# Experts' weight ring: the eleven early buffers first, loaded unit by unit during the output projection

## The chip, the core and the metric

The kernel runs on one NeuronCore of a Trainium2 chip, as one launch. The metric is the device time of that core in microseconds, taken as the median of several executions. The engines named below are TensorE (PE; PEld is its weight load), VectorE (DVE), ScalarE (ACT), GpSimd (POOL) and SyncE (SP), which here only issues DMAs. Each engine works through its own list of instructions in order, so an instruction that waits holds up all that stand behind it on the same engine.

## What is computed

Two transformer blocks in a row on 512 tokens of width 1024. The change touches the last part of the second block: the output projection of the token mixer, the second norm, and a mixture of 32 experts of which each token uses two. Cut to that:

```python
def second_block(x, c, ...):
    ...
    x = x + g1 * token_mixer(h, ...)              # ends in: merged @ w_out
    h = rms_norm(x, norm2_g) * (1.0 + sc2) + sh2
    x = x + g2 * hier_moe(h, ...)
    return rms_norm(x, final_g)

def hier_moe(h, w_group, b_group, w_expert, b_expert, w_gate, w_up, w_down):
    g_prob = softmax(h @ w_group + b_group)       # 4 groups, best one
    e_logits = h @ w_expert + b_expert            # 8 experts of that group, best two
    ...
    def expert_block(xb, e):
        return (silu(xb @ w_gate[e]) * (xb @ w_up[e])) @ w_down[e]
```

All in float32. An expert has three matrices (gate and up 1024x256, down 256x1024) of 1.05 MB each, 32 experts have 96 of them.

## The kernel before

**Stages.** `block2` runs the second block. Its last stages are `Moe.mix_out` (output projection, residual, norm, router logits), `Moe.route` (which token goes to which expert, by one-hot matmuls) and `Moe.run` (the experts). The 32 experts are taken as 16 pairs, then one block for an expert with more than 64 tokens (the "far" block, the thirteenth in the order, three matrices), so 17 blocks with 99 matrices.

**The ring of weights.** Each matrix is loaded into one unit of 128x2048 float32, by one DMA on SP's queue. There are 18 units, which `Moe.raw` hands out in turn: `NR = 5, 11` says that the first 5 come from the pool `er2`, the next 11 from the pool `er`, and the last 2 are the halves of `x`, the residual stream, which is free once its rows are stored. `er` is opened in `Moe.__init__`, before the output projection. `er2` can be opened only when the projection's input `m_hi`, `m_lo` has been read (`mst.close()`), and `block2` puts it at the head of the list. A pair needs 6 units: gate, gate, up, up, down, down. With 18 units three pairs fit; from the nineteenth load on a unit must be given back by the pair three places earlier: gate and up when `up` of that pair is through on PE, down when `down` is.

**Loads.** `Moe.load` takes the units of a pair at once, first gate and up of both experts and then both down, so in the first pair five units are of `er2` and one (a down) is of `er`. The first pair is asked for in `Moe.open`, the next two at the head of `Moe.run`. The loads of the third pair are placed behind `self.hold`. At the first load that comes round to a used unit, POOL clears two words of it (`memset`), placed behind the first gather.

**Hold.** `self.hold` is a small DMA on SP's queue that stores one column (128 words) of the first gathered block. It waits for the first gather, so SP issues nothing behind it until that has landed.

**Gather.** The normed tokens are stored to `hd` in DRAM, four stores of 128 rows, the last one at the end of `mix_out`. The first gather (POOL, indirect) reads rows of `hd` and so waits for all four stores and for the indices. The three blocks that gathers fill, `xg`, and the tiles `h` that are stored to `hd` rotate through the same three buffers `wraw`; the fourth `h` takes the buffer of the first.

**Order.** The order on each engine is made by a scheduler when the kernel is built; `tc.issue_after(i)` keeps what is written under it behind instruction `i`. `declare_no_dep` and the rest are untouched here. DMAs of SP take turns on eight completion semaphores, so an issue also waits until the transfer eight issues earlier has landed.

Of the kernel before, what the change touches and what calls it, by code (L numbers as in the profile page):

```python
# [9 lines left out]
F32 = mybir.dt.float32  # L10
# [1879 lines left out]
NE = 32  # L1890
# [1 line left out]
FAR = 128  # L1892
NPAIR = NE // 2
NOV = 15
NR = 5, 11
NX = 3
AHEAD = 2
FAR_AT = 12
# [6 lines left out]
class Moe:  # L1905
# [3 lines left out]
    def __init__(self, K, st):  # L1909

        nc, i = K.nc, K.i
        self.K, self.sc = K, []
        P = lambda *a, **k: st.enter_context(K.pool(*a, **k))
        cp = self.cp = P(name="ec", bufs=1, side="right")
        self.x = cp.tile([128, NT, D], F32, name="xres2")
        self.ss = cp.tile([128, 2, NT], F32, name="ss2")
        self.er = [P(name="er", bufs=NR[1], side="right")]
        self.nraw = 0
        self.first = None
        self.cst = cp.tile([128, ECOLS], F32, name="ecst")  # L1920
        nc.sync.dma_start(self.cst, i["ce"])
        self.xa = K.dram.tile([T, D], F32, name="xa")

        self.yd = K.dram.tile([2 * T, D], F32, name="yd")
# [11 lines left out]
    def mix_out(self, xd, mod, m_hi, m_lo):  # L1936

        K, cp, x, ss = self.K, self.cp, self.x, self.ss
        nc, i = K.nc, K.i
# [5 lines left out]
        with K.pool(name="mo", bufs=2) as wp:  # L1945
# [56 lines left out]
            def logits1(t):  # L2002
                ps = K.aux()
                for k in range(4):
                    s = slice(k * 128, (k + 1) * 128)
                    nc.tensor.transpose(ps[:, s], x[:, t, 512 + k * 128:640 + k * 128], K.ident)
                h = K.wraw()
                late = t >= NT - 2
                (nc.vector if t == NT - 1 else nc.gpsimd).tensor_mul(h, x[:, t, :], G)
                v = K.col(1, "msv")  # L2010
                nc.vector.tensor_add(v, ss[:, 0, t:t + 1], ss[:, 1, t:t + 1])
                nc.vector.tensor_scalar(v, v, RS / D, RS * 1e-6, op0=OP.mult, op1=OP.add)
                xT = rot([128, 512], "xT")
                nc.scalar.copy(xT, ps)
                rs = K.rsqrt(v, 1)
                nc.vector.scalar_tensor_tensor(l0[:, t], l0[:, t], rs, bias, op0=OP.mult, op1=OP.add)
                pl = K.aux()
                for k in range(4):
                    nc.tensor.matmul(pl[:, :36], xT[:, k * 128:(k + 1) * 128], wr[:, 4 + k, :],
                                     start=k == 0, stop=k == 3)  # L2020
                nc.vector.scalar_tensor_tensor(self.lg[:, t], pl[:, :36], rs, l0[:, t], op0=OP.mult, op1=OP.add)
                if late:

                    dg = rot([128, 128], "dg")
                    nc.scalar.activation(dg, K.ident, AF.Copy, scale=rs)
                    for s in HALF:
                        ps = K.mm()
                        nc.tensor.matmul(ps, dg, h[:, s], start=True, stop=False)
                        nc.tensor.matmul(ps, K.ident, sh2[:, s], start=False, stop=True)
                        nc.scalar.copy(h[:, s], ps)  # L2030
                else:
                    nc.scalar.activation(h, h, AF.Copy, scale=rs)
                    nc.gpsimd.tensor_add(h, h, sh2)
                nc.sync.dma_start(self.hd[t * 128:(t + 1) * 128, :], h)

            wt = []
            for u in range(4):
                raw = K.wraw()
                r3 = raw.rearrange("p (k n) -> p k n", k=2)
                nc.sync.dma_start(r3, w[u * 256:(u + 1) * 256, 512:].rearrange("(k p) n -> p k n", p=128))  # L2040
                wt.append(K.split(raw, pool=None if u < 3 else wp, bufs=3 if u < 3 else 1))
            for t in range(NT):
                if t == 1:
                    logits0()
                if t > 1:
                    logits1(t - 2)
                ps = K.mm()
                for k in range(8):
                    hi, lo = (a[:, (k % 2) * 512:(k % 2 + 1) * 512] for a in wt[k // 2])
                    tt = slice(t * 128, (t + 1) * 128)  # L2050
                    nc.tensor.matmul(ps, m_hi[:, k, tt], hi, start=k == 0, stop=False)
                    nc.tensor.matmul(ps, m_hi[:, k, tt], lo, start=False, stop=False)
                    nc.tensor.matmul(ps, m_lo[:, k, tt], hi, start=False, stop=k == 7)
                residual(1, t, ps)
# [3 lines left out]
    def route(self):  # L2058
        K, cp = self.K, self.cp
        nc, tc, i = K.nc, K.tc, K.i  # L2060
# [13 lines left out]
        with K.pool(name="eh", bufs=2, side="right") as hp, ExitStack() as late:  # L2074
# [89 lines left out]
            q1 = places(rk, iota, "roh")  # L2164
            at = index(idx[:, :NPAIR], slots(q1, hb)[:, :NPAIR], T).ins
            self.gather(self.xg[0], idx[:, 0:1])

            self.hold = nc.sync.dma_start(K.dram.tile([128, 1], F32, name="hold"), self.xg[0][:, 0:1]).ins
            late.enter_context(tc.issue_after(at))

            def softmax(src, m, n, nm):
# [86 lines left out]
    def gather(self, xb, ixc):  # L2258

        nc = self.K.nc  # L2260
        at = nc.gpsimd.indirect_dma_start(out=xb, out_offset=None, in_=self.hd,
                                          in_offset=bass.IndirectOffsetOnAxis(ap=ixc, axis=0),
                                          bounds_check=T - 1, oob_is_err=False)
        self.first = self.first or at.ins

    def load(self, *experts):

        nc = self.K.nc
        rw = [[self.raw() for _ in range(2)] for _ in experts]
        rw = [(*a, self.raw()) for a in rw]  # L2270
        for a, b, n in [(a, b, n) for n in range(3) for a, b in zip(rw, experts)]:
            if self.wrap and self.nraw > sum(NR) + 2:
                with self.K.tc.issue_after(self.first):
                    nc.gpsimd.memset(a[n][:, 0:512:256], 0.0)
                self.wrap = False
            nc.sync.dma_start(a[n], b[n])
        return rw

    def spread(self, xb):

# [55 lines left out]
    def open(self, st, mod):  # L2336
        K = self.K
        self.g2 = bcast(K, st.enter_context(K.pool(name="ef", bufs=1)), mod["g2"], "g2row")
        self.wp = st.enter_context(K.pool(name="ew", bufs=2))
        self.xg = [K.wraw() for _ in range(NX)]  # L2340
        self.wrap = True
        flat = lambda a, k: a.rearrange("e (p k) n -> e p (k n)", k=k)
        self.wd = [flat(K.i[n][0], k) for n, k in (("moe_w_gate_2", 8), ("moe_w_up_2", 8), ("moe_w_down_2", 2))]

        self.order = [8 * a + e for e in range(8) for a in range(2)]
        self.order.insert(FAR_AT, None)
        self.ready = [self.weights(0)]

    def weights(self, n):
        q = self.order[n]  # L2350
        if q is None:
            e = self.K.nc.sync.value_load(self.ove[0:1, 0:1], min_val=0, max_val=NE - 1)
            return self.load([a[bass.ds(e, 1)].rearrange("o p n -> p (o n)") for a in self.wd])
        e = q // 8 * 16 + q % 8
        return self.load(*([a[e + 8 * h] for a in self.wd] for h in range(2)))

    def run(self, st, out):
        K = self.K
# [7 lines left out]
        for j in range(n):  # L2366
            if j + AHEAD < n:
                self.gather(xg[(j + AHEAD) % NX], col(self.idx, j + AHEAD))
            while len(self.ready) <= min(j + 2, n - 1):
                with tc.issue_after(self.hold) if len(self.ready) == 2 else ExitStack():  # L2370
                    self.ready.append(self.weights(len(self.ready)))
            th = self.up(xt, self.ready[j])
            if j + 1 < n:
                xt = self.spread(xg[(j + 1) % NX])
            self.down(th, self.ready[j], col(self.wsl, j), col(self.dst, j))
# [10 lines left out]
        with tc.For_i(0, nov, 1) as b:  # L2386
            for o, a in ((ixd, self.idx), (dsd, self.dst), (wd_, self.wsl)):
                nc.vector.tensor_copy(o, a[:, bass.ds(b + NPAIR + 1, 1)])
            er = nc.sync.value_load(self.ove[0:1, bass.ds(b + 1, 1)], min_val=0, max_val=NE - 1)
            self.gather(xg[0], ixd)  # L2390
            rw = self.load([a[bass.ds(er, 1)].rearrange("o p n -> p (o n)") for a in self.wd])
            self.down(self.up(self.spread(xg[0]), rw), rw, wd_, dsd)

        ssf = K.col(8, "ssf")
# [92 lines left out]
def block2(K, x, B, mats, mod, out):  # L2487
# [30 lines left out]
    with ExitStack() as st:  # L2518
        moe = Moe(K, st)
        moe.mix_out(xd, mod, m_hi, m_lo)  # L2520
        mst.close()
        moe.er.insert(0, st.enter_context(K.pool(name="er2", bufs=NR[0])))
        moe.open(st, mod)
        moe.route()
        moe.run(st, out)
# [69 lines left out]
```

## Time and profile before

| | us |
|---|---|
| median of 3 runs | 1680.52 |
| the three runs | 1680.20, 1680.52, 1682.46 |
| the profiled execution | 1682.32 |
| its span, first to last instruction | 1680.5 |
| PE busy in the span | 1570.6 (93%) |
| DMA, mean over the span | 169 GB/s |

The page cuts the span into 40 slices of 42 us. PE is the busy engine nearly all the way, and the DMA engines are mostly not: their share and rate differ by stage. The last eight slices (from 1344 us) are the end of the output projection, routing, the experts, and the final norm. A wait is put down by the trace to the one of several releasers that came last.

### The profile page before, as it was taken

To read this page: it belongs to the slowest core of one execution; us is meant where nothing else is said; L and a number is where in the kernel's file an instruction comes from. 1 tells how busy PE (TensorE), PEld (TensorE's weight loads), DVE (VectorE), ACT (ScalarE), POOL (GpSimd) and SP (SyncE) were. 2 spreads that over 40 slices of the span, in tenths; PEclk is the share of its full clock that TensorE was granted. 3 is DMA by queue.
4 is the path that set the end of the run, shared out by engine and by line. 5 is a ranking of instruction groups with operands and counts; after the bars stand their busy time and mean duration, and the time that the engine had idled before them with its cause. 6 is when DMAs were issued, how large, how long until landed. Compare 5 with 4: busy or idle time off the path is not lost. (4 is left out here: it accounts for less than half of the span.)

```text
span 1680.5 us, 25313 instructions
## 1 busy us (share of the span) xinstructions
PE 1570.6 (93%) x9568; PEld 1173.1 (70%) x9568; DVE 933.7 (56%) x2155; ACT 636.2 (38%) x1300; POOL 235.7 (14%) x271
## 2 busy tenths in 40 slices
PE   6999999999999999999999999999999979989981
PEld 5777777778777887778787667676678755544550
DVE  6764367568989876455666545555434472221114
ACT  4543337554322332345443455555642321000001
POOL 1212221100000000004210112112202221110102
PEclk9999999999999999999999999999999989999996
DMA  5221121137468866326854212111127759999994
GB/s 151 64 76 51 52 101 64 63 103 216 148 203 210 203 225 192 113 76 198 173 123 143 77 45 64 51 57 57 32 97 254 291 221 336 418 418 419 419 396 176
DMA packets 204306, 284.74 MB, mean 169 GB/s; under 512 B 75667, under 2 KB 150422, under 8 KB 191510
## 3 DMA queue, kind: packets, MB, share of 16 engines
q1 hardware_dynamic: 198370, 273.07, 49.2%
q0 software_dynamic: 4896, 8.40, 1.3%
q10 hardware_dynamic: 915, 1.64, 0.3%
q8 instruction: 76, 1.25, 0.3%
q14 instruction: 49, 0.39, 0.1%
HBM read 262.07 MB, written 30.43 MB: 174 GB/s over the span
## 5 line engine op out<-in xcount | busy, mean ns | idle before, releaser
L154 DVE TENSOR_TENSOR wlo<-wraw,whi 128x1024 fp32r<-128x1024 f32 x162 | 204.2, 1262 | 156.2 <-ACT whi L153 155.5
L153 ACT CAST whi<-wraw 128x1024 fp32r<-128x1024 f32 x164 | 171.8, 1050 | 243.7 <-PE mm L1055 71.9
L213 PE MATMUL mm<-hhi,whi 128*128 128x512 f32 x440 | 184.3, 419 | 5.4 <-DVE mx L1757 2.9
L215 PE MATMUL mm<-hhi,wlo 128*128 128x512 f32 x440 | 176.6, 402 | 0.1
L214 PE MATMUL mm<-hlo,whi 128*128 128x512 f32 x440 | 176.2, 401 | 0.0
L2302 PE MATMUL mm<-eraw,xt 128*64 128x256 f32 (+1 forms) x1024 | 128.3, 382 | 10.8 <-DMA eraw<-in_moe_w_up 7.3
L171 PE MATMUL mm<-hhi,whi 128*128 128x512 f32 x320 | 127.4, 398 | 0.3 <-ACT whi L153 0.3
L172 PE MATMUL mm<-hlo,whi 128*128 128x512 f32 x320 | 126.3, 395 | 0.0
L173 PE MATMUL mm<-hhi,wlo 128*128 128x512 f32 x320 | 125.9, 395 | 0.0
L2302 PEld LDWEIGHTS mm<-eraw,xt 128*64 128x64 f32 (+1 forms) x1024 | 84.5, 139 | 49.9 <-DMA eraw<-in_moe_w_up 10.5
L213 PEld LDWEIGHTS mm<-hhi,whi 128*128 128x128 f32 x440 | 83.1, 189 | 32.5 <-issue 8.3
L215 PEld LDWEIGHTS mm<-hhi,wlo 128*128 128x128 f32 x440 | 83.1, 189 | 20.6 <-issue 1.6
L214 PEld LDWEIGHTS mm<-hlo,whi 128*128 128x128 f32 x440 | 83.1, 189 | 18.7 <-issue 4.7
L1760 ACT ACTIVATE NP<-NP,mx 128x512 f32<-128x512 f32 (+3 forms) x128 | 72.1, 564 | 44.3 <-DVE mx L1757 43.7
L1757 DVE CUSTOM_DVE_ANT_0 NP<-mm,ncst 128x512 f32<-128x512 f32 (+3 forms) x128 | 61.4, 480 | 37.5 <-PE aux L1788 35.9
L2328 DVE SCALAR_TENSOR_TENSOR ey<-mm,wsl,g2row 128x512 f32<-128x512 f32 x34 | 25.5, 751 | 85.8 <-PE mm L2324 85.8
L171 PEld LDWEIGHTS mm<-hhi,whi 128*128 128x128 f32 x320 | 60.2, 188 | 15.5 <-issue 0.8
L1054 PE MATMUL mm<-wlo,ahi 128*128 128x512 f32 x176 | 69.2, 393 | 1.4 <-DVE wlo L154 1.4
L173 PEld LDWEIGHTS mm<-hhi,wlo 128*128 128x128 f32 x320 | 60.2, 188 | 14.2
L172 PEld LDWEIGHTS mm<-hlo,whi 128*128 128x128 f32 x320 | 60.3, 188 | 13.6
L1053 PE MATMUL mm<-whi,ahi 128*128 128x512 f32 x176 | 69.7, 400 | 0.0
L1055 PE MATMUL mm<-whi,alo 128*128 128x512 f32 x176 | 69.5, 395 | 0.0
(787 smaller groups left out, 3285.7 us busy)
## 6 DMA issues: line engine op xcount, KB each, us to landing
wraw<-in_w_in SPq DMA_DIRECT2D x68, 512.0 KB
eraw<-in_moe_w_gate SPq DMA_DIRECT2D x32, 1024.0 KB
eraw<-in_moe_w_up SPq DMA_DIRECT2D x32, 1024.0 KB
eraw<-in_moe_w_down SPq DMA_DIRECT2D x25, 1024.0 KB
araw<-in_ada_w SPq DMA_DIRECT2D x48, 512.0 KB
wraw<-in_w_gate SPq DMA_DIRECT2D x22, 512.0 KB
wraw<-in_w_up SPq DMA_DIRECT2D x22, 512.0 KB
wraw<-in_w_down SPq DMA_DIRECT2D x22, 512.0 KB
```

The lines of the kernel that those rows point to most:

```text
L153: nc.scalar.copy(hi[:, :m], raw[:, :m])
L154: (eng or nc.vector).tensor_sub(lo[:, :m], raw[:, :m], hi[:, :m].bitcast(F32))
L171: nc.tensor.matmul(o, hi[:, k, a:a + m], xhi[:, kk, :], start=kk == 0, stop=False)
L172: nc.tensor.matmul(o, hi[:, k, a:a + m], xlo[:, kk, :], start=False, stop=False)
L173: nc.tensor.matmul(o, lo[:, k, a:a + m], xhi[:, kk, :], start=False, stop=kk == nk - 1)
L213: nc.tensor.matmul(ps, hi, xhi[:, k, :], start=k == 0, stop=False)
L214: nc.tensor.matmul(ps, hi, xlo[:, k, :], start=False, stop=False)
L215: nc.tensor.matmul(ps, lo, xhi[:, k, :], start=False, stop=k == nk - 1)
L1053: nc.tensor.matmul(ps, a[:, tt], hi[:, k, :], start=kk == 0, stop=False)
L1055: nc.tensor.matmul(ps, b[:, tt], hi[:, k, :], start=False, stop=kk == cn - 1)
L1760: nc.scalar.activation(p[:, :n], p[:, :n], AF.Exp, scale=-1.0, bias=m, accum_out=d)
L2302: nc.tensor.matmul(ph[n][s], xt[:, k, s], r[n][:, k * 256:(k + 1) * 256], start=k == 0, stop=k == 7)
```

## The change

`NR` becomes `11, 5`: the first 11 units are those of `er`, the next 5 those of `er2` (now put behind `er` in the list), the last 2 still the halves of `x`. `load` becomes a generator that takes one unit and issues its DMA at a time; `weights` chains the pairs, and `fetch(n)` runs it until n units have been taken. The places at which units are asked for are: 11 in `mix_out`, just ahead of the loop over the four row blocks; 2 more in `open`; 3 more there behind the last store to `hd`; the 2 halves of `x` behind the hold; all others in `run`, as before, when a block is due. The `memset` of POOL is gone. Matrices, their order and the number of loads are the same.

```diff
-NR = 5, 11
+NR = 11, 5
...
-                nc.sync.dma_start(self.hd[t * 128:(t + 1) * 128, :], h)
+                self.stored = nc.sync.dma_start(self.hd[t * 128:(t + 1) * 128, :], h).ins
...
+            self.fetch(NR[0])
             for t in range(NT):
                 if t == 1:
                     logits0()
...
-            self.hold = nc.sync.dma_start(K.dram.tile([128, 1], F32, name="hold"), self.xg[0][:, 0:1]).ins
+            hold = nc.sync.dma_start(K.dram.tile([128, 1], F32, name="hold"), self.xg[0][:, 0:1]).ins
+            with tc.issue_after(hold):
+                self.fetch(sum(NR) + 2)
...
     def load(self, *experts):
 
         nc = self.K.nc
-        rw = [[self.raw() for _ in range(2)] for _ in experts]
-        rw = [(*a, self.raw()) for a in rw]
-        for a, b, n in [(a, b, n) for n in range(3) for a, b in zip(rw, experts)]:
-            if self.wrap and self.nraw > sum(NR) + 2:
-                with self.K.tc.issue_after(self.first):
-                    nc.gpsimd.memset(a[n][:, 0:512:256], 0.0)
-                self.wrap = False
-            nc.sync.dma_start(a[n], b[n])
-        return rw
+        rw = [[] for _ in experts]
+        for n in range(3):
+            for r, e in zip(rw, experts):
+                r.append(self.raw())
+                nc.sync.dma_start(r[n], e[n])
+                yield
+        self.ready.append(rw)
...
+    def fetch(self, units):
+
+        while self.nraw < units:
+            next(self.loads)
...
-        self.ready = [self.weights(0)]
...
+        self.fetch(NR[0] + 2)
+        with K.tc.issue_after(self.stored):
+            self.fetch(sum(NR))
...
-            while len(self.ready) <= min(j + 2, n - 1):
-                with tc.issue_after(self.hold) if len(self.ready) == 2 else ExitStack():
-                    self.ready.append(self.weights(len(self.ready)))
+            while len(self.ready) <= min(j + 2, n - 1) and next(self.loads, self) is None:
+                pass
...
-        moe.er.insert(0, st.enter_context(K.pool(name="er2", bufs=NR[0])))
+        moe.er.append(st.enter_context(K.pool(name="er2", bufs=NR[1])))
```

On SP's queue in the output projection, before (`eraw` is a unit of the ring, `xres` the tile `x`, `xa` and `hd` the stores of the residual and of the normed rows):

```order
L2276 DMA eraw<-in_moe_w_down 128x2048
L2040 DMA wraw<-in_w_out 128x2x512 x3
L2276 DMA eraw<-in_moe_w_gate 128x2048 x2
L2276 DMA eraw<-in_moe_w_up 128x2048 x2
L2276 DMA eraw<-in_moe_w_down 128x2048
L1960 DMA xa<-xres_12812 128x1024
L2276 DMA eraw<-in_moe_w_down 128x2048
L2034 DMA hd<-wraw 128x1024
L1960 DMA xa<-xres_12812 128x1024
```

And after the change, the same stretch:

```order
L2280 DMA eraw<-in_moe_w_gate 128x2048
L2045 DMA wraw<-in_w_out 128x2x512 x3
L2280 DMA eraw<-in_moe_w_gate 128x2048
L2280 DMA eraw<-in_moe_w_up 128x2048 x2
L2280 DMA eraw<-in_moe_w_down 128x2048 x2
L2280 DMA eraw<-in_moe_w_gate 128x2048 x2
L2280 DMA eraw<-in_moe_w_up 128x2048 x2
L2280 DMA eraw<-in_moe_w_down 128x2048
L1965 DMA xa<-xres_12812 128x1024 x2
L2039 DMA hd<-wraw 128x1024
```

Eleven units stand ahead of the first store instead of six (seven ahead of the second), and the second `xa` store now stands ahead of the first `hd` store.

On SP's queue around the last `hd` store and the hold, before:

```order
L2034 DMA hd<-wraw 128x1024
L2276 DMA eraw<-in_moe_w_gate 128x2048
L2034 DMA hd<-wraw 128x1024
L2276 DMA eraw<-in_moe_w_gate 128x2048
L2276 DMA eraw<-in_moe_w_up 128x2048 x2
L2276 DMA eraw<-in_moe_w_down 128x2048
L2168 DMA hold<-wraw 128x1
L2276 DMA eraw<-in_moe_w_gate 128x2048 x2
L2276 DMA eraw<-in_moe_w_up 128x2048 x2
L2276 DMA xres_12812<-in_moe_w_down 128x2048 x2
L2276 DMA eraw<-in_moe_w_gate 128x2048 x2
```

And after:

```order
L2039 DMA hd<-wraw 128x1024
L2280 DMA eraw<-in_moe_w_down 128x2048
L2039 DMA hd<-wraw 128x1024
L2280 DMA eraw<-in_moe_w_gate 128x2048 x2
L2280 DMA eraw<-in_moe_w_up 128x2048 x2
L2173 DMA hold<-wraw 128x1
L2280 DMA xres_12812<-in_moe_w_down 128x2048 x2
L2280 DMA eraw<-in_moe_w_gate 128x2048 x2
L2280 DMA eraw<-in_moe_w_up 128x2048 x2
```

One unit ahead of the last `hd` store and four behind it stand in both. Behind the hold six units stood before the first reused one (the four `eraw` rows and the two `xres`); now two do, the halves of `x`.

On PE in the seventh pair (`L2302`/`L2322` are the matmuls of `up`, `L2324`/`L2344` those of `down`, `ident,wraw` the transposes of the next block), before:

```order
L2302 MATMUL mm<-eraw,xt 64x256 x32
L2316 MATMUL aux<-ident,eth 128x128 x2
L2288 MATMUL aux<-ident,wraw 128x128 x4
L2324 MATMUL mm<-eraw,ea 64x512 x2
L2288 MATMUL aux<-ident,wraw 128x128
L2324 MATMUL mm<-eraw,ea 64x512 x6
L2288 MATMUL aux<-ident,wraw 128x128 x3
```

And after:

```order
L2322 MATMUL mm<-eraw,xt 64x256 x32
L2308 MATMUL aux<-ident,wraw 128x128 x4
L2336 MATMUL aux<-ident,eth 128x128 x2
L2308 MATMUL aux<-ident,wraw 128x128 x4
L2344 MATMUL mm<-eraw,ea 64x512 x8
L2308 MATMUL aux<-ident,wraw 128x128 x3
```

In the sixth and the seventh pair the transposes no longer stand between the matmuls of `down`; from the eighth pair's `down` on both kernels have the same rows.

The scheduler also moved one DVE instruction: the multiply that makes the fourth `h` (L2009, now L2014) stands three short instructions later, inside the chain that makes the fourth row block's norm factor. Between the sixth and the eighth pair two copies of a gathered block on DVE and one gather on POOL change places with a neighbour.

## Rows read from the trace of the kernel before

**Rows 1.** Page, 40 slices of 42 us: DMA share in tenths, GB/s moved.
```profile
DMA  5221121137468866326854212111127759999994
GB/s 151 64 76 51 52 101 64 63 103 216 148 203 210 203 225 192 113 76 198 173 123 143 77 45 64 51 57 57 32 97 254 291 221 336 418 418 419 419 396 176
```

**Rows 2.** Windows of 20 us: busy us by engine, clock, DMA share, GB/s.
```profile
1340.00:1360.00 20.00, 19.23 (x95) 14.70 (x95) 11.96 (x32) 5.26 (x11) 9.31 (x4) 1.00 0.27 106
...
1600.00:1620.00 20.00, 19.42 (x131) 11.41 (x131) 4.29 (x7) 1.34 (x3) 1.94 (x2) 1.00 1.01 419
```

**Rows 3.** Windows of 4 us, columns as in Rows 2, around gather and hold.
```profile
1332.00:1336.00 4.00, 3.92 (x20) 2.17 (x19) 2.64 (x3) 1.63 (x4) 1.83 (x1) 1.00 0.39 145
...
1384.00:1388.00 4.00, 2.78 (x14) 2.65 (x14) 1.30 (x6) 0.00 (x0) 0.00 (x0) 0.50 0.84 333
...
1392.00:1396.00 4.00, 4.00 (x38) 2.93 (x39) 0.33 (x3) 0.00 (x0) 0.78 (x1) 1.00 0.47 39
...
1396.00:1400.00 4.00, 4.00 (x36) 2.68 (x30) 0.84 (x2) 0.67 (x2) 0.32 (x2) 1.00 0.93 388
```

**Rows 4.** Timeline of SP: start us, us, queue, line, transfer, how many issues.
```profile
1342.18 0.33 SPq L2034 DMA_DIRECT2D hd<-wraw  x1
...
1346.56 0.33 SPq L1960 DMA_DIRECT2D xa<-xres  x1
...
1365.93 0.37 SPq L2276 DMA_DIRECT2D eraw<-in_moe_w_gate  x1
...
1371.21 0.32 SPq L2034 DMA_DIRECT2D hd<-wraw  x1
...
1374.14 1.09 SPq L2276 DMA_DIRECT2D eraw<-in_moe_w_down  x1
...
1387.01 0.33 SPq L2168 DMA_DIRECT2D hold<-wraw  x1
...
1389.56 1.52 SPq L2276 DMA_DIRECT2D xres<-in_moe_w_down  x2
...
1398.38 1.85 SPq L2276 DMA_DIRECT2D eraw<-in_moe_w_gate  x2
...
1504.50 2.81 SPq L2276 DMA_DIRECT2D eraw<-in_moe_w_up  x2
...
1509.48 2.81 SPq L2276 DMA_DIRECT2D eraw<-in_moe_w_down  x2
```

**Rows 5.** Timeline of PE in the expert loop; brackets: idle before, and releaser.
```profile
1388.94 1.99 PE L2302 MATMUL mm<-eraw,xt 128*64 128x256 f32 x10
...
1404.84 7.08 PE L2302 MATMUL mm<-eraw,xt 128*64 128x256 f32 x64
...
1417.43 7.08 PE L2302 MATMUL mm<-eraw,xt 128*64 128x256 f32 x64
...
1478.46 3.67 PE L2302 MATMUL mm<-eraw,xt 128*64 128x256 f32 x30 [1.19 <-DMA eraw<-in_moe_w_up]
...
1495.30 3.67 PE L2302 MATMUL mm<-eraw,xt 128*64 128x256 f32 x30 [1.26 <-DMA eraw<-in_moe_w_up]
...
1586.26 7.12 PE L2302 MATMUL mm<-eraw,xt 128*64 128x256 f32 x62
...
1601.19 7.18 PE L2302 MATMUL mm<-eraw,xt 128*64 128x256 f32 x64
...
1630.61 3.67 PE L2302 MATMUL mm<-eraw,xt 128*64 128x256 f32 x32 [1.64 <-DMA eraw<-in_moe_w_gate]
...
1636.10 3.67 PE L2302 MATMUL mm<-eraw,xt 128*64 128x256 f32 x30 [1.82 <-SPq L2386]
```

**Rows 6.** Timeline of DVE and POOL around the routing stage.
```profile
1361.50 1.22 DVE L2009 TENSOR_TENSOR wraw<-xres,G 128x1024 f32<-128x1024 f32 x1
...
1378.41 1.23 POOL L2261 DMA_INDIRECT wraw<-hd,idx  x1 [10.56 <-DVE sgd L2176]
...
1398.25 0.10 POOL L2274 MEMSET eraw<- 128x2 f32 x1 [2.03 <-PE mm L2302]
```

More of the change, by code (lines that the diff above doesn't have):

```diff
@@ L1916, in __init__ @@
         self.ss = cp.tile([128, 2, NT], F32, name="ss2")
-        self.er = [P(name="er", bufs=NR[1], side="right")]
+        self.er = [P(name="er", bufs=NR[0], side="right")]
         self.nraw = 0
-        self.first = None
+        flat = lambda a, k: a.rearrange("e (p k) n -> e p (k n)", k=k)
+        self.wd = [flat(i[n][0], k) for n, k in (("moe_w_gate_2", 8), ("moe_w_up_2", 8), ("moe_w_down_2", 2))]
+        self.order = [8 * a + e for e in range(8) for a in range(2)]
+        self.order.insert(FAR_AT, None)
+        self.ready, self.loads = [], self.weights()
         self.cst = cp.tile([128, ECOLS], F32, name="ecst")
@@ L2263, in gather, with weights @@
                                           bounds_check=T - 1, oob_is_err=False)
-        self.first = self.first or at.ins
+        return at.ins
     def load(self, *experts):
         nc = self.K.nc
-        rw = [[self.raw() for _ in range(2)] for _ in experts]
-        rw = [(*a, self.raw()) for a in rw]
-        for a, b, n in [(a, b, n) for n in range(3) for a, b in zip(rw, experts)]:
-            if self.wrap and self.nraw > sum(NR) + 2:
-                with self.K.tc.issue_after(self.first):
-                    nc.gpsimd.memset(a[n][:, 0:512:256], 0.0)
-                self.wrap = False
-            nc.sync.dma_start(a[n], b[n])
-        return rw
+        rw = [[] for _ in experts]
[5 more added lines that the diff above has]
+        self.ready.append(rw)
+    def weights(self):
+        for q in self.order:
+            if q is None:
+                e = self.K.nc.sync.value_load(self.ove[0:1, 0:1], min_val=0, max_val=NE - 1)
+                yield from self.load([a[bass.ds(e, 1)].rearrange("o p n -> p (o n)") for a in self.wd])
+            else:
+                e = q // 8 * 16 + q % 8
+                yield from self.load(*([a[e + 8 * h] for a in self.wd] for h in range(2)))
+    def fetch(self, units):
+        while self.nraw < units:
+            next(self.loads)
     def spread(self, xb):
@@ L2340, in open @@
         self.xg = [K.wraw() for _ in range(NX)]
[L2341 to L2346, printed above, removed]
-        self.ready = [self.weights(0)]
[L2349 to L2355, printed above, removed]
+        self.fetch(NR[0] + 2)
+        with K.tc.issue_after(self.stored):
+            self.fetch(sum(NR))
     def run(self, st, out):
@@ L2390, in run @@
             self.gather(xg[0], ixd)
-            rw = self.load([a[bass.ds(er, 1)].rearrange("o p n -> p (o n)") for a in self.wd])
+            list(self.load([a[bass.ds(er, 1)].rearrange("o p n -> p (o n)") for a in self.wd]))
+            rw = self.ready[-1]
             self.down(self.up(self.spread(xg[0]), rw), rw, wd_, dsd)
```

## The prediction

> **What bounds the kernel now.** I read the page's slices first. In the last eight the DMA engines change from mostly idle to saturated: 221 GB/s in the slice from 1344 us, 336 in the next, then 418, 418, 419, 419 and 396 [rows 1]. So the expert loop lives on its transfers, and the end of the projection and the routing do not: from 1340 to 1360 us the share is 0.27 and the rate 106 GB/s, against 1.01 and 419 late in the loop [rows 2].
>
> Next the timeline of PE, to see whether the saturation is what the loop waits for. An early pair, whose matrices are there already, takes 1417.43 - 1404.84 = 12.6 us. A later one takes 1495.30 - 1478.46 = 16.8 us and stops before its second half for a DMA of an `up` matrix (1.19 and 1.26 us idle; the rest of the difference is the transposes set between `down`'s matmuls). Pairs after the far block, with those transposes and no such wait, take 1601.19 - 1586.26 = 14.9 us. The last pair stops twice, 1.64 us for its gates and 1.82 us before its second half; the second is put down to SP's branch, but what these matmuls read are the `up` units [rows 5]. So the DMA stream sets the end of the loop, and PE has 16.8 - 14.9 = 1.9 us to spare in a pair of the slow form, 4.2 in one of the fast form.
>
> Then where the stream begins. SP issues the hold at 1387.01, when the first gather has landed, and the six fresh units behind it by 1391 [rows 4]. But the engines move 333 GB/s up to 1388, 39 GB/s between 1392 and 1396, and 388 in the next 4 us [rows 3]. On SP's queue the 128 four-byte rows of the hold come first, and the weights behind it start only near 1396.3 (388 of 419 GB/s over those 4 us means full rate for 3.7 of them). From there to the last matrices it never stops [rows 1]. Before that, the queue ran empty at about 1332.5 (145 GB/s in the window 1332 to 1336 [rows 3]) and stayed nearly so until the unit at 1365.93.
>
> **The price of a unit.** SP issues each load when the one eight places ahead has landed, so in the saturated loop its pace is the DMA pace: the two `up` loads start at 1504.50, the two `down` loads at 1509.48 [rows 4], 4.98 us for two units with no gather between, 2.49 us each. That is 1.05 MB / 2.49 us = 421 GB/s, which fits the 419.
>
> The Trainium skill (DMA: Bandwidth & Descriptors, section Bandwidth) measures a single 1 MB transfer at 6.15 us, 341 GB/s. By that rate four units would be 12.3 us and the time 1668.2; here transfers stand in a queue one behind the other, and the trace's 419 GB/s decides.
>
> **The change, part by part.**
>
> *Units moved ahead of the hold.* Before, 7 + 5 = 12 of the 18 fresh units stood on SP's queue ahead of the hold; in the changed order 11 + 5 = 16 do. Behind it stand 87 of the 99 matrices before, 83 after. The stream from 1396.3 to the end is therefore shorter by 4 x 2.49 = 10.0 us. The four units are carried in the hole between 1332.5 and 1366, which has room for (1366 - 1332.5) x 0.73 / 2.49, nine units, after its other traffic (0.27 of the engines [rows 2]).
>
> *Around the last `hd` store and the gather.* One unit stands ahead of that store and four behind, in both kernels (issued at 1365.93, and between 1371.21 and 1375.2 [rows 4]). The first gather is issued at 1378.41 [rows 6], its landing and the hold at 1387.01 share the engines with the same five units. Cost 0; I find no reason for a gain either, since the rest that the gather waits for is the routing chain.
>
> *Reuse of the first unit.* The first reused unit was issued at 1398.38 [rows 4], as `up` of the first pair ended on PE and the memset (0.10 us at 1398.25 [rows 6]) was through. It will again be issued near 1398.4. Before, that was hidden behind six units of queue (1396.3 + 6 x 2.49 = 1411.2). Now only two stand ahead, so the cover ends at 1396.3 + 2 x 2.49 = 1401.3, 2.9 us after the issue. Enough, with a cost between 0 and about 1 us if the issue needs longer to reach the engines; I take 0. The next four follow in the same way: `down` of the first pair frees its units near 1405 (the next `up` begins at 1404.84 [rows 5]) and they are needed at 1401.3 + 4 x 2.49 = 1411.3; `up` of the second pair frees four at 1404.84 + 7.08 = 1411.9, needed from 1416.3 on. The lead is 3 to 6 us at first, and grows, as PE needs 12.6 us for a pair and DMA 16.8. The memset's removal is worth 0 to 0.2 us.
>
> *Stores behind more weights.* This is where the change could cost. SP's first `xa` store now stands behind eleven units rather than six, and the first `hd` store behind the second `xa` store, so it is issued just after 1346.56 rather than at 1342.18 [rows 4]. The queue that ran empty at 1332.5 now does so five units later: 1332.5 + 5 x 2.49 = 1345 at full rate, or 1332.5 + 5 x 1.05 / 0.291 = 1350.5 at the 291 GB/s of that whole slice [rows 1]. Add two `xa` stores and the `hd` store, half a unit each: landed by 1350 to 1356. Who waits for it is the multiply on DVE that writes the fourth `h` into the buffer of the first, at 1361.50 [rows 6]. Cost 0, with 5 to 11 us in hand. The later stores are issued at the same times but for half a microsecond, since they wait for their data.
>
> *The moved DVE multiply.* It lasts 1.22 us [rows 6] and now stands inside the fourth block's norm chain, so that chain ends up to 1.2 us later, and the multiply itself by about as much as the three short instructions last. The last `hd` store needs both, and their sum on DVE is the same. Between 0 and 1.2 us; I take 0.
>
> *PE.* The first pair's weights come earlier than before, but its `up` already started at 1388.94 [rows 5], 1.9 us after the hold was issued, as the gathered block was transposed: 0. Two more pairs get the fast form. That is no gain while DMA sets the pace.
>
> **The sum.** Profiled: span 1680.5 - 10.0 = 1670.5, and that execution's own time 1682.3 - 10.0 = 1672.3. The profiled execution stands 1.8 us above the median of the runs; the median becomes 1680.5 - 10.0 = 1670.5 us. With the bounds: 10.0 - 1.0 - 1.2 = 7.8 us at the least by these terms, 10.2 at the most, and 1 to 2 us for the spread of the runs.
>
> **Rivals.**
>
> *A. PE takes over, part of the gain is lost.* For: with DMA 10 us ahead, PE waits less, and the slow form is not far from the DMA pace. Against: the sixth pair starts at 1417.43 + 3 x 12.6 = 1455.2 in either kernel; from there PE alone needs two fast pairs and then the slow form, 1455.2 + 2 x 12.6 + 4 x 14.9 = 1540 for the twelfth pair's start and near 1544 for its second half, where DMA before allowed 1495.30 + 4 x 16.8 = 1562.5 and now would allow 1552.5 [rows 5]. After the far block PE is the slower one, but it only carries on from there, and the last pair still has 1.64 + 1.82 us of waits to give. If PE lost 3 to 4 us more than that: 1674.
>
> *B. No change.* The early units flow, but gather and hold land 10 us later, through the longer backlog on SP's queue; the stream then restarts 10 us later with 10 us less to do: 1680. Against: the hole drains by 1350, and the five units about the last store are the same.
>
> *C. Slower.* Place: the first `hd` store behind the weights. If it landed after 1361.50, DVE would stand at the fourth multiply with the whole routing chain queued behind it, and gather and hold would move by as much. It decides from 10.0 us late (no gain) and shows as slower from 13.4 us late, a landing at 1375. The queue's work began at about 1332.5 - 7.5 x 2.49 = 1314 (six units and three half-size loads of the projection's weights). If the eleven units and those loads went at half the steady rate, 12.5 x 2.49 / 0.5 = 62 us, the queue would empty at 1376 and the `hd` store, with two stores ahead of it, land at about 1379, 17.5 us late: 1688. For: the hold shows how a transfer on this queue keeps those behind it waiting, 39 GB/s for four of its eight microseconds [rows 3]. Against: the slice in which they lie moved 291 GB/s with the hole in it [rows 1], and even at that rate the slack is 5 us.
>
> The Trainium skill (DMA: Bandwidth & Descriptors, section Queues, rings and completion order) gives the same mechanism: each engine takes SP's descriptors in ring order and shares only between queues. It speaks against long loads ahead of stores on one queue. By that rule the first stores are late by five units, as worked out above; the trace agrees as far as the hold goes.
>
> **How the numbers follow.** Forecast (all or nearly all of the 10 us): 0.80. A: 0.08. B: 0.05. C: 0.07. The measurement tells some 0.2%, 3.4 us, from no change. Faster by more than that: forecast and A, 0.88. Same: B, 0.05. Slower: C, 0.07. The range runs from 1667 (a restart up to 1 us sooner, the gather a little sooner, and the spread of the runs) to 1676, which takes in the bounds and A; it leaves out B and C.
>
> **What would show it.** Right: in the changed trace the DMA rate between 1332 and 1345 stays near 419 GB/s; the hold is issued near 1387; behind it two units, then the first reused one at about 1398.4, and no dip in the rate from 1397 on; the waits of later pairs for `up` matrices begin two or three pairs later; the last `down` of PE and all behind it stand 10 us earlier. Wrong: a dip after 1401 (reuse sets the stream); a DVE gap at the fourth multiply, or the hold later than 1388 (rival B or C); pairs at 14.9 us to the end without waits for DMA (rival A).

## The result: 10 us forecast, 8.4 us measured

The changed kernel takes 1671.82 us in the median of 5 runs (1668.38 to 1672.8), the kernel before 1680.2 us beside it (5 runs, 1677.71 to 1682.46). The ratio is 0.9948, with a 95% interval from 0.9933 to 0.9963. A second measurement (e9 below) gave 1669.96 against 1679.05, ratio 0.9951 [0.9938, 0.9965]. The forecast was 1670.5, in a range of 1667 to 1676.

The profiled execution has a span of 1671.0 us (time 1672.8), 9.5 us less than before. The slices of the page, which answer to [rows 1] (columns of 41.8 us; a row of DMA busy tenths, then the rate):

```profile
span 1671.0 us, 25319 instructions
...
DMA  4221121137467967325863322111127869999994
GB/s 147 69 77 52 52 102 64 64 88 211 148 216 205 210 214 216 103 89 165 177 154 113 89 64 64 51 40 56 45 75 265 302 256 326 418 418 418 419 397 178
```

The plateau at 418 GB/s is as high as before. Where it begins shows in windows of 4 us (columns as in [rows 2]; the last two are the DMA share and GB/s):

```profile
1332.00:1336.00 4.00, 3.92 (x20) 2.26 (x19) 2.56 (x3) 1.55 (x4) 1.74 (x1) 1.00 1.01 420
1336.00:1340.00 4.00, 3.02 (x10) 1.07 (x8) 2.21 (x11) 1.60 (x3) 0.74 (x2) 1.00 1.01 420
1340.00:1344.00 4.00, 3.67 (x15) 2.16 (x16) 0.26 (x1) 1.13 (x3) 2.24 (x1) 1.00 1.01 420
...
1352.00:1356.00 4.00, 4.00 (x25) 3.38 (x24) 3.21 (x3) 1.55 (x4) 3.04 (x2) 1.00 0.00 0
...
1388.00:1392.00 4.00, 4.00 (x24) 2.73 (x23) 1.36 (x4) 0.59 (x1) 0.00 (x0) 0.71 1.04 50
1392.00:1396.00 4.00, 4.00 (x39) 3.01 (x40) 0.33 (x3) 0.00 (x0) 0.00 (x0) 1.00 0.43 29
1396.00:1400.00 4.00, 4.00 (x36) 2.67 (x33) 0.51 (x2) 0.38 (x1) 0.99 (x1) 1.00 0.75 301
1400.00:1404.00 4.00, 3.65 (x23) 1.91 (x23) 1.35 (x3) 1.45 (x3) 0.99 (x1) 1.00 1.01 413
```

The hole from 1332 is filled with weights (420 where [rows 3] has 145), the queue runs empty by 1352, and the trough behind the hold is as deep as before (29 against 39). The stream restarts a little later: 301 GB/s in the window from 1396, where [rows 3] has 388. That is (388 - 301) x 4 / 419 = 0.8 us: by these rates the stream is back at 1396.3 us before and at 1397.1 in the changed kernel.

SP's timeline, which answers to [rows 4] (start, us, queue, line, transfer, count):

```profile
1334.06 12.91 SPq L1965 DMA_DIRECT2D xa<-xres  x2
1347.07 0.38 SPq L2039 DMA_DIRECT2D hd<-wraw  x1
...
1371.29 0.32 SPq L2039 DMA_DIRECT2D hd<-wraw  x1
1371.66 1.78 SPq L2280 DMA_DIRECT2D eraw<-in_moe_w_gate  x2
1373.49 1.75 SPq L2280 DMA_DIRECT2D eraw<-in_moe_w_up  x2
1387.27 0.33 SPq L2173 DMA_DIRECT2D hold<-wraw  x1
1387.69 0.85 SPq L2280 DMA_DIRECT2D xres<-in_moe_w_down  x2
1398.55 0.82 SPq L2280 DMA_DIRECT2D eraw<-in_moe_w_gate  x2
```

Two units stand behind the hold instead of six, and the first reused unit is issued at 1398.55, 0.17 us from where it was.

PE's timeline answers to [rows 5] (brackets: idle before, and releaser):

```profile
1389.20 2.06 PE L2322 MATMUL mm<-eraw,xt 128*64 128x256 f32 x10
...
1502.66 3.67 PE L2322 MATMUL mm<-eraw,xt 128*64 128x256 f32 x30 [1.09 <-DMA eraw<-in_moe_w_up]
...
1621.29 3.67 PE L2322 MATMUL mm<-eraw,xt 128*64 128x256 f32 x32 [1.65 <-DMA eraw<-in_moe_w_gate]
1626.78 3.67 PE L2322 MATMUL mm<-eraw,xt 128*64 128x256 f32 x30 [1.82 <-SPq L2394]
```

The last pair waits as long as before (1.65 and 1.82 us), but 9.32 us earlier than in [rows 5]. DMA still sets the end.

### The profile page after: what moved, and what is told of

It is laid out like the page before. It is cut to its first block, busy times and chain, and to the rows that moved or that the text cites. A ratio compares the mean times of both kernels' runs of the same rounds, so it can differ in the third digit from the quotient of the medians.

```text
span 1671.0 us, 25319 instructions
## 1 busy us (share of the span) xinstructions
PE 1564.5 (94%) x9568; PEld 1171.6 (70%) x9568; DVE 933.6 (56%) x2155; ACT 635.6 (38%) x1300; POOL 235.7 (14%) x270
## 5 line engine op out<-in xcount | busy, mean ns | idle before, releaser
L2322 PE MATMUL mm<-eraw,xt 128*64 128x256 f32 (+1 forms) x1024 | 126.8, 382 | 7.2 <-DMA eraw<-in_moe_w_up 3.6
L2322 PEld LDWEIGHTS mm<-eraw,xt 128*64 128x64 f32 (+1 forms) x1024 | 84.2, 139 | 46.4 <-DMA eraw<-in_moe_w_up 5.6
```

What stands on the lines that cost most here:

```text
L2322: nc.tensor.matmul(ph[n][s], xt[:, k, s], r[n][:, k * 256:(k + 1) * 256], start=k == 0, stop=k == 7)
```

## The experiments

**A measure that is steadier than the time.** The runs of one kernel lie up to some 5 us to either side of their median, and one cause is seen in the traces: the last `hd` store, which the whole program up to the output projection leads to, is issued at 1371.29 us in one profile of the changed kernel and at 1366.55 in the other (e9). So beside the medians I give the distance from that store to the second half of the last pair (in the trace above 1626.78 - 1371.29 = 255.49). For the two kernels with two profiles each these differ in it by 0.6 and 1.0 us. The medians were taken in four groups, in which the kernel before took 1680.2 us (changed), 1679.22 (e1 to e4), 1681.21 (e5 to e8) and 1679.05 (e9 to e11); each ratio is to the kernel before in the same group. "Row" is a hold that stores one row of 128 numbers, "column" the original one.

| kernel | units ahead | hold | hold issued after last `hd` store, us | last pair after it, us | median, us | ratio to before [95%] |
|---|---|---|---|---|---|---|
| before | 12 | column | 15.80 | 264.89 | 1680.2 | 1 |
| changed | 16 | column | 15.98, 15.91 | 255.49, 256.10 | 1671.82, 1669.96 | 0.9948 [0.9933, 0.9963] |
| e1 | 12 | row | 15.80 | 258.78 | 1671.73 | 0.9952 [0.9935, 0.9969] |
| e2 | 12 | column | 11.74 | 260.20 | 1675.30 | 0.9977 [0.9966, 0.9987] |
| e3 | 16 | row | 15.45 | 258.22 | 1670.42 | 0.9944 [0.9924, 0.9964] |
| e4 | 16 | column | 15.91 | 255.63 | 1671.65 | 0.9953 [0.9934, 0.9971] |
| e5, e10 | 14 | column | 11.85, 11.68 | 256.90, 255.90 | 1670.27, 1671.61 | 0.9934 [0.9916, 0.9951], 0.9954 [0.9940, 0.9967] |
| e11 | 15 | column | 13.60 | 255.49 | 1668.71 | 0.9941 [0.9927, 0.9954] |
| e7 | 12 | row | 11.89 | 254.34 | 1668.92 | 0.9923 [0.9907, 0.9938] |
| e6 | 14 | row | 11.43 | 252.97 | 1667.12 | 0.9914 [0.9901, 0.9928] |

The traces also give the price of a unit by itself. If the restart of the stream is reckoned as above, the last pair follows it by 239.8 and 239.6 us with twelve units ahead of the column hold (before, e2), by 235.4 and 235.2 with fourteen (e5, e10), by 232.3 with fifteen (e11) and by 229.7, 230.0 and 229.9 with sixteen (changed, e9, e4). Four units are worth 9.6 to 10.2 us there. The rest of what these runs differ by is when the stream restarts.

**e2: the four units behind the hold again.** In the changed kernel, one unit beyond the eleven goes ahead, the rest follows the hold:

```
-        self.fetch(NR[0] + 2)
-        with K.tc.issue_after(self.stored):
-            self.fetch(sum(NR))
+        self.fetch(NR[0] + 1)
```

> The changed kernel, with the four units that stood between the last hd store and the hold moved behind the hold: 12 units ahead of it as in the kernel before, 6 behind. Ring order and the eleven early units stay. Theory (the time goes by the number of units left behind the hold and by when the hold ends): four units more behind it cost 10.0 us, and the first gather, no longer sharing the engines with them, may land up to 5 us sooner, so 1676 to 1682. Rival (the gain comes from the ring's order, from the first pair's early weights or from the moved PE rows and not from the count): about 1672.

Measured 1675.30, 3.9 us below the kernel before in its group (1679.22). It lies just under the range of the theory and 3 us above the rival. From the restart on the missing units cost what they should (1627.67 - 1388.1 = 239.6 us to the last pair, against 239.8 before), but something came back ahead of it, and the trace shows what (SP, the window of the restart and the last pair on PE, then POOL's first gather):

```profile
1367.47 0.32 SPq L2039 DMA_DIRECT2D hd<-wraw  x1
1379.21 0.32 SPq L2173 DMA_DIRECT2D hold<-wraw  x1
```

```profile
1388.00:1392.00 4.00, 4.00 (x38) 2.78 (x39) 0.34 (x3) 0.00 (x0) 0.99 (x1) 1.00 0.98 406
```

```profile
1627.67 3.67 PE L2322 MATMUL mm<-eraw,xt 128*64 128x256 f32 x30 [1.80 <-SPq L2392]
```

```profile
1374.68 1.23 POOL L2268 DMA_INDIRECT wraw<-hd,idx  x1 [10.56 <-DVE sgd L2183]
```

From the gather's issue to the hold it is 1379.21 - 1374.68 = 4.53 us here, 1387.27 - 1378.50 = 8.77 in the changed kernel and 1387.01 - 1378.41 = 8.60 before. The four units that both of those have in front of the gather slow it by 4.1 to 4.2 us. e2 lacks them, so its hold comes 4.1 us sooner after the last `hd` store (11.74 against 15.80), and its last pair 264.89 - 260.20 = 4.69 us sooner than before.

**e1: the kernel before with another hold.** The hold must read what the gather wrote, but one row of it will do:

```
-  self.hold = nc.sync.dma_start(K.dram.tile([128, 1], F32, name="hold"), self.xg[0][:, 0:1]).ins
+  self.hold = nc.sync.dma_start(K.dram.tile([1, 128], F32, name="hold"), self.xg[0][0:1, 0:128]).ins
```

> The kernel before with one edit: the hold stores 128 words of one row of the first gathered block instead of one word of each of its 128 rows; it still waits for the same gather, and the six fresh units still stand behind it. The PE order is that of before. Theory (the stream of weights from the hold on sets the end, and the hold's small pieces keep SP's queue busy from 1387 to 1396): the stream restarts at 1388 to 1389 instead of 1396.3, the six units cover the wait for the first reuse at 1398.4, so 7 to 8 us faster, about 1672.5. Rival (the gain of the changed kernel comes from the two pairs of PE with the transposes out of the way, or from the first pair's weights being early): neither is touched here, so 1680.

Measured 1671.73 against 1679.22, 7.5 us less, as the theory has it. With no unit moved at all, the trough is gone (windows of 4 us):

```profile
1388.00:1392.00 4.00, 4.00 (x17) 2.14 (x16) 1.36 (x4) 0.59 (x1) 0.99 (x1) 0.50 0.93 341
1392.00:1396.00 4.00, 4.00 (x19) 3.55 (x21) 0.33 (x3) 0.00 (x0) 0.00 (x0) 0.50 1.02 415
...
1404.00:1408.00 4.00, 3.65 (x24) 2.15 (x24) 1.28 (x3) 1.45 (x3) 0.99 (x1) 1.00 0.96 356
```

The hold is issued at 1386.85, 15.80 us after the last `hd` store as before. So the prediction read the trough rightly: it is the 128 four-byte pieces in front of the weights that hold the stream up, not the gather and not PE. The Trainium skill (DMA: Bandwidth & Descriptors, section Specifications) puts the shortest transfer that runs at line rate at 512 bytes. The trace agrees in kind. From the hold's issue to the full rate it is 1396.3 - 1387.0 = 9.3 us with the column; with the same 512 bytes in one row it is 1.15 us up to 1388 and (419 - 341) x 4 / 419 = 0.7 us of the window after it, 1.9 in all. That is 7.4 us less, but in the trace the last pair comes only 264.89 - 258.78 = 6.1 us sooner. Of the difference, (419 - 356) x 4 / 419 = 0.6 us is the dip in the window from 1404: in this profile the first pair was slow (its clock is at 0.50, see e3), and the first reused unit was issued 16.2 us after the hold (1403.07 - 1386.85) instead of 11.4. The other 0.7 us stays open.

**e3: both, the changed kernel with the row hold.** The edit of e1 in the changed kernel.

> The changed kernel with the one-row hold; PE order unchanged. Theory: with only two units behind the hold the stream is then limited by the first reuse, which waits for the first pair's up (issue near 1398.5, stream full near 1400 instead of 1402), so only about 2 us faster than the changed kernel: 1670. Rival (the hold's 8 us are simply part of the sum and come back in full): 1664.

Measured 1670.42, the time that the theory gives, and no better than the changed kernel beyond the noise (the intervals overlap). Its profile isn't faster at all: the last pair comes 258.22 us after the last `hd` store, 2.7 us later than in the changed kernel. The stream restarts at once and then stands still (windows of 4 us; the third number from the end is the granted clock):

```profile
1388.00:1392.00 4.00, 4.00 (x18) 3.49 (x16) 0.00 (x0) 0.00 (x0) 0.00 (x0) 0.50 0.79 323
1392.00:1396.00 4.00, 4.00 (x21) 2.27 (x22) 0.33 (x3) 0.00 (x0) 0.00 (x0) 0.50 0.00 0
1396.00:1400.00 4.00, 4.00 (x37) 2.60 (x34) 0.00 (x0) 0.00 (x0) 0.00 (x0) 0.94 0.00 0
1400.00:1404.00 4.00, 3.66 (x24) 2.23 (x23) 1.53 (x3) 1.83 (x4) 0.99 (x1) 1.00 0.84 279
```

Two units behind the hold last 5 us. Then the ring waits for the first buffer that is used again, which is free when `up` of the first pair ends on PE. This is the reuse wait that the prediction put at 0 for the changed kernel. In this profile the first pair was also slow, its clock at 0.50 (1.2 GHz) until about 1396, and the unit was issued 1399.65 - 1383.76 = 15.9 us after the hold, against 11.3 in the changed kernel. That accounts for most of the 2.7 us. But even at 11.3 the stream would have stood for about 11.3 - 1.9 - 5.0 = 4.4 us, an estimate from these rows; e6 below shows the wait with the clock up. It is hidden in the changed kernel only because the column hold takes as long: 9.9 us from the hold to the restart and 5.0 for two units are more than 11.3.

**e4: without the fetch in the projection.** The line `self.fetch(NR[0])` ahead of the loop over blocks is taken out; the same units are then requested only where `open` asks for them, and the scheduler places them.

> The changed kernel without the request for eleven units inside the output projection: the same eleven are asked for after it, and the order built from that spreads them between the xa and hd stores; 16 units still stand ahead of the hold, 2 behind, PE order unchanged. Theory (only the count ahead of the hold matters, the hole in the projection has room either way): the same as the changed kernel, 1671 to 1673. Rival (loading them early and in one go is what pays, or units among the stores delay the gather): 3 us or more slower, 1675 to 1680.

Measured 1671.65, last pair at 255.63: as the changed kernel. With sixteen units ahead of the hold, it doesn't matter where in the projection they are asked for.

**e5: fourteen ahead, four behind.** Two units instead of four after the last `hd` store:

```
-        self.fetch(NR[0] + 2)
+        self.fetch(NR[0] + 1)
         with K.tc.issue_after(self.stored):
-            self.fetch(sum(NR))
+            self.fetch(NR[0] + 3)
```

> The changed kernel with two of the four units behind the last hd store moved behind the hold: 14 units ahead, 4 behind; the hold as it is. Theory (units behind the hold cost 2.49 us each, and each unit beside the first gather delays its landing by about 1.05 us, as 12 ahead showed: hold 4.2 us sooner after the last store for four units): 5.0 - 2.1 = 2.9 us slower than the changed kernel, between it and 12 ahead, 1673 to 1675. Rival (count alone, the gather's landing does not move): 5 us slower, 1676.5.

Measured 1670.27. Both missed: it is not slower than the changed kernel beyond the noise (in the trace the last pair comes 0.8 to 1.4 us later). I had taken it that two units slow the gather by half of what four do. They hardly slow it: the hold follows the last `hd` store by 11.85 us, as with no units (11.74). What is lost by two units behind the hold (5.0 us) is nearly won back by the earlier hold (15.98 - 11.85 = 4.1 us).

**e6 and e7: fourteen and twelve ahead, with the row hold.** These are e5 and e2 with e1's edit of the hold.

> 14 units ahead and the one-row hold. Theory: the hold falls 2.1 us sooner, the stream restarts at once, four fresh units cover 10 us, and the first reuse is 11 to 16 us behind the hold, by how soon TensorE's clock rises in the first pair; so the stream reaches the first reused unit 0 to 4 us sooner than in the changed kernel: 1668 to 1671. Rival (each unit behind the hold costs 2.49 us whatever the hold is): 1675.

> 12 units ahead and the one-row hold. Theory: the hold falls 4.2 us sooner, the stream restarts at once, and six fresh units cover 15 us, so that the first reuse hardly binds; the first reused unit is reached about 2 us sooner than in the changed kernel: 1669 to 1670, with 12 units ahead as in the kernel before, whose 1680 the rival (the count ahead of the hold sets the time) expects.

Measured 1667.12 and 1668.92: e7 at the lower end of the theory's range, e6 0.9 us under it. By the traces the last pair comes 2.5 to 3.1 us sooner than in the changed kernel in e6 and 1.2 to 1.8 sooner in e7, as the theory has it. e6 is faster than both kernels of this case: ratio 0.9914 [0.9901, 0.9928] against 0.9948 [0.9933, 0.9963] for the changed one. e7 shows that the wait for reuse goes as soon as there are enough units behind the hold. Its windows (the first fence) have no dip, those of e6 (the second) one that costs three to four microseconds, where the ring waits for the first pair:

```profile
1388.00:1392.00 4.00, 4.00 (x38) 2.91 (x39) 0.33 (x3) 0.00 (x0) 0.00 (x0) 1.00 1.02 419
1392.00:1396.00 4.00, 4.00 (x34) 2.68 (x30) 0.84 (x2) 0.69 (x2) 0.00 (x0) 1.00 1.01 420
```

```profile
1388.00:1392.00 4.00, 4.00 (x39) 3.16 (x40) 0.33 (x3) 0.00 (x0) 0.00 (x0) 1.00 1.01 415
1392.00:1396.00 4.00, 4.00 (x36) 2.52 (x33) 0.21 (x1) 0.38 (x1) 0.00 (x0) 1.00 0.31 100
1396.00:1400.00 4.00, 3.66 (x24) 2.20 (x24) 1.33 (x3) 1.45 (x3) 0.99 (x1) 1.00 0.89 350
```

At twelve units ahead the row hold is worth 260.20 - 254.34 = 5.9 us here and 264.89 - 258.78 = 6.1 us in the kernel before.

**e9 to e11: sixteen, fourteen and fifteen ahead on one chip, column hold.** e9 is the changed kernel itself, e10 is e5 again, e11 asks for one unit more:

```
-            self.fetch(NR[0] + 3)
+            self.fetch(NR[0] + 4)
```

> The changed kernel itself, on the same chip as the other two of this group: 16 units ahead of the hold, 2 behind. The trace of its first profile has the hold 16.0 us after the last hd store and the second half of the last pair 255.5 us after that store. Expected: the same two figures within 0.5 us, and 1671 to 1672 in the median.

> Fourteen units ahead, four behind, the column hold, once more, to be set against the changed kernel on one chip. In the first look its median was 1.5 us below that of the changed kernel, while in its trace the last pair came 1.4 us later after the last hd store (256.9 against 255.5). By the trace: hold 11.9 us after the last hd store, last pair near 256.9, median 1 to 2 us above the changed kernel. By the medians (the rival): 1 to 2 us below it, and the last pair then at 255 or less.

> Fifteen units ahead, three behind, the column hold. Theory (only what is still on its way when the gather is issued, 6.8 us after the last hd store, delays the gather; two units are through about then, and cost it 0.1 us): a third unit holds it up for one unit's time at the most, hold 12.9 to 14.4 us after the last hd store; last pair 1.0 to 2.5 us later through that and 2.5 us earlier through the shorter stream, so 255.4 to 256.9, median as e10 or up to 1.5 us below. Rival (the gather suffers as a whole as soon as anything stands in its way): hold at 15.5 to 16.0 as with four units, last pair near 258, 2.5 us later than with sixteen ahead.

Medians 1669.96, 1671.61 and 1668.71, last pair at 256.10, 255.90 and 255.49. e9 narrowly misses two of its figures: the last pair is 0.6 us off where 0.5 was expected at most, and the median 1 us under its range. e10's median stands 1.65 us above e9's, as the trace of e5 had it, but its own last pair does not stand later; the two kernels differ by less than one profile of them does from the next. e11's last pair is as expected, its median 1.4 us lower than expected. For the gather e11 decides (SP, then POOL):

```profile
1368.27 0.32 SPq L2039 DMA_DIRECT2D hd<-wraw  x1
...
1381.87 0.33 SPq L2173 DMA_DIRECT2D hold<-wraw  x1
```

```profile
1375.49 1.23 POOL L2268 DMA_INDIRECT wraw<-hd,idx  x1 [10.57 <-DVE sgd L2183]
```

The hold comes 13.60 us after the last `hd` store (theory 12.9 to 14.4, rival 15.5 to 16.0), and the gather takes 6.38 us to the hold, between 4.63 with two units (e10) and 8.84 with four (e9). So only what is still under way when the gather is issued, 7 us after that store, slows it, the third unit by 1.8 us and the fourth by 2.5. A unit takes 2.49 us. The fifteenth and sixteenth unit thus give back in the gather nearly what they save in the stream. By the last pair 14, 15 and 16 ahead lie within 0.6 us of each other in these three traces, and within 1.4 us with e5 and the first profile of the changed kernel.

The Trainium skill (DMA: Bandwidth & Descriptors, section Queues, rings and completion order) says that an engine takes turns between the queues that have work for it. The trace agrees that they share: the gather is on another queue than the weights and still lands 4.1 to 4.2 us later when four of them are there. How the turns are taken no run here shows.

**e8: no reloads at all.** `run` takes the buffers of the first three groups again instead of loading, and `load` puts a group on the list before its units are asked for:

```
+        self.ready.append(rw)
         for n in range(3):
...
-        self.ready.append(rw)
...
-            while len(self.ready) <= min(j + 2, n - 1) and next(self.loads, self) is None:
-                pass
+            while len(self.ready) <= min(j + 2, n - 1):
+                m = len(self.ready)
+                self.ready.append(self.ready[m % 3][:1 if order[m] is None else 2])
```

> The changed kernel without the 81 loads that come after the first 18: pairs four to seventeen use the matrices of the first three pairs again, so the output is not the reference's; the hold, the gathers, the scatters and all matmuls stay. All pairs have the fast form on PE in this order of instructions. It measures how far PE alone could go. Theory (DMA sets the end, PE has room): PE at 12.6 us a pair starts the last pair near 1594 instead of 1619 and does not stop in it, so 24 to 28 us faster than the changed kernel, 1644 to 1648. Rival (PE was about to take over, the changed kernel has used up nearly all room): 1664 to 1670.

Measured 1645.03 (4 runs), ratio 0.9779 [0.9759, 0.9799]: the theory. PE alone, with all pairs in the fast form, ends some 27 us before the changed kernel does. PE is busy and the DMA engines nearly idle (windows of 40 us):

```profile
1420.00:1460.00 40.00, 38.58 (x283) 21.78 (x283) 8.94 (x16) 4.98 (x11) 6.54 (x7) 1.00 0.15 42
...
1500.00:1540.00 40.00, 38.59 (x292) 22.23 (x290) 9.56 (x16) 4.02 (x9) 7.09 (x7) 1.00 0.10 32
```

## Why the prediction was right, point by point

*What bounds the kernel* held. e8 takes the reloads away and the time falls by some 27 us. e1 changes only the form of the hold, the trough goes, and it gains 7.5 us in the median (6.1 by the trace).

*Four units at 2.49 us* held: 9.6 to 10.2 us from the restart of the stream on, where 10.0 was said. The last pair stands 9.32 us earlier, or 9.40 counted from the last `hd` store (8.79 in the second profile, e9). The trace has the rest: the stream restarts 0.8 us later, and 0.26 us of that is the hold's later issue. The prediction let it restart at the same time. The medians' 8.4 and 9.1 us differ from these figures by less than the runs of one kernel spread. POOL shows the later landing of the hold, since the next gather on its queue waits for it (before: 1395.22, after 12.26 us of wait):

```profile
1396.31 0.99 POOL L2268 DMA_INDIRECT wraw<-hd,idx  x1 [13.89 <-DMA hold<-wraw]
```

From the hold's issue to the restart it is 9.3 us before and 9.9 here. In the nine profiles with the column it lies between 8.9 (e2) and 10.2 us (e9), so half a microsecond need not come from the change; what sets it no run shows.

*The price of the stores behind eleven units* was rightly put at 0, and that of the moved multiply too. The first `hd` store is issued at 1347.07, between `xa` stores, and the queue is empty from 1352, ten microseconds ahead of the multiply that could have waited for it. The multiply on DVE doesn't wait for it; it comes behind three short instructions, as the moved code says (DVE):

```profile
1362.55 1.23 DVE L2014 TENSOR_TENSOR wraw<-xres,G 128x1024 f32<-128x1024 f32 x1
```

It stands 1.05 us later than in [rows 6], the last `hd` store 0.08 us later. So rival C, which needed that store to land after 1361.50, did not come about.

*Around the gather* 0 was right, and for the reason given: the same number of units stands in front of the gather in both kernels, and from its issue to the hold it takes 8.60 and 8.77 us. But the prediction, which says that landing and units share the engines, put no price on that. "I find no reason for a gain either" is true of this change alone: fewer units there would have brought up to 4.2 us, as e2 shows. My forecast of e5 then spread this price evenly over the four units, and e11 shows that only those still under way count.

*Reuse* at 0 held with little to spare, as said. The unit is issued at 1398.55, some 3.5 us before the two units behind the hold are through (1397.1 + 5.0), and the window from 1400 moves 413 GB/s. e3 shows the wait once the cover is gone.

*PE (rival A)* took nothing. The pairs' waits for `up` matrices on PE fell from 6 to 3 (all waits of PE for them between 1384 and 1640 us: total, times, longest; before, then after):

```profile
PE mm L2302 <- DMA eraw<-in_moe_w_up: 7.3, 6, 1.4
```

```profile
PE mm L2322 <- DMA eraw<-in_moe_w_up: 3.6, 3, 1.4
```

The last pair's waits are unchanged, and the first wait for `up` moved from 1461.69 to 1502.66 us, from the sixth pair to the ninth, where two or three pairs were forecast. *Rival B* (hold 10 us later) is refuted by the hold at 1387.27.

## What to carry to other kernels

Where a saturated load stream sets the end, what counts is how many bytes stand behind the point where it last stood still; each unit moved ahead of it is worth its own transfer time, until something else on the same engines is delayed by it. So look at what is under way when the small transfer on the critical path is issued, and at what the small transfer itself keeps waiting: here a 512-byte store cost 6 us, as much as nearly two and a half loads of a megabyte each. Gains on one gap don't simply add up: with the hold mended, the ring's first reuse became the wait, and of the three counts tried with it fourteen units ahead came out best, not sixteen (the intervals of these three runs still touch).

## What the runs showed of the hardware

- A store of 128 pieces of four bytes kept the weights behind it on SP's queue at 29 to 52 GB/s for some 8 us (before, changed); 128 numbers of one row did not (e1, 341 GB/s and more). Taking the column away was worth 5.9 and 6.1 us by the traces (e2 to e7, before to e1), less than the length of the trough.
- From the issue of the gather of one block from DRAM to the hold it took 4.5 and 4.7 us with no unit asked for behind the last `hd` store (e2, e7), 4.2 to 5.0 with two, asked for some 7 us ahead of the gather (e6, e10, e5), 6.4 with three (e11) and 8.6 to 8.8 with four (before, changed, e9).
- The granted clock during the first pair's `up` differs between executions. In the first profiles of both kernels it rises from 0.50 (1.2 GHz) to 1.00 (2.4 GHz) at about 1390 us, 1 us after those matmuls start. In e1, e3 and e8 PE had waited 1.2 us for the gather, in the kernel before too, and yet the clock stayed at 0.50 for some 10 us after the start, with PE busy throughout. The last 54 matmuls of `up` then took 8.62 us in e1, 8.45 in e3 and 8.60 in e8, against 6.26 in the changed kernel, and in e1 and e3 the first reused unit was issued 16.2 and 15.9 us after the hold, against 11.4 and 11.3 in the two kernels. The kind of hold is not what decides it: e8 has the column, and e6 and e7 have the row and the early rise. What does is open.
